# Second layer's modulation vectors by multiply-and-add on VectorE and a matmul against ones

## The chip, the cores and the metric

The kernel runs on one core of one Trainium2 chip. The metric is the device time of one execution in microseconds (us), given as the median of several runs. The engines have short names in the profile: PE is TensorE's matmul, PEld its weight load, DVE VectorE, ACT ScalarE, POOL GpSimd, SP the engine whose queue issues most of the loads.

## The reference

The program is two trunk layers over 512 latent tokens and 256 context tokens, width 1024, all in fp32. Each layer first turns two condition vectors (one for the latent stream, one for the context stream) into six modulation vectors of 1024 numbers per stream:

```python
def modulation(cvec, w_mod, b_mod):
    m = (jax.nn.silu(cvec) @ w_mod + b_mod)[..., None, :]
    return jnp.split(m, 6, axis=-1)

sh1, sc1, ga1, sh2, sc2, ga2 = modulation(c, w_mod, b_mod)
sh1c, sc1c, ga1c, sh2c, sc2c, ga2c = modulation(c_ctx[None], w_mod, b_mod)
u = (rmsnorm(x, g_mix) * (1 + sc1) + sh1) @ w_in
uc = (rmsnorm(cx, g_mix) * (1 + sc1c) + sh1c) @ w_in
...
x = x + ga1 * mix
x = x + ga2 * squared_relu_mlp(rmsnorm(x, g_mlp) * (1 + sc2) + sh2, w_up, w_down)
if update_ctx:      # all layers but the last
    ...             # the same two lines for cx, with ga1c, sc2c, sh2c, ga2c
return x, cx
```

So the modulation is a vector of 1024 numbers times a matrix of 1024 x 6144, for each of two streams, 25 MB of weights a layer. In the second layer the context needs its first shift and scale alone (sh1c, sc1c), because its tokens are not updated there.

## The kernel before

The two layers run one after the other: norm and input projection, three mixing groups, output projection, then the MLP (hidden width 4096, in eight blocks of 512). Every projection on TensorE takes three fp32r matmuls per tile (high by high, high by low, low by high), so each weight tile is loaded raw by SP, rounded to its high part on ACT (line 144), and its low part is the difference on DVE (line 68, called from 145). The raw tiles have three buffers, the high parts five (tag "hi"), the low parts five (tag "lo").

The second layer's modulation is computed during the first layer's MLP. A generator, `mod_all` (361), makes three rounds of 2048 columns: round 0 gives the first shift and scale, round 1 ga1 and the second shift, round 2 the second scale and ga2. `modulation_round` (166) has eight steps in each round, one per tile of 128 rows of w_mod (k). A step loads two tiles of 128 x 1024 (512 KB each) into a "hi" and a "lo" buffer and issues four fp32 matmuls of 512 columns, one for each 32 columns of the array: stationary is a 128 x 32 tile in which columns 0 and 1 hold the two activated condition vectors (`sstat`), moving is the weight tile. The four sums lie on four groups of 32 partitions of one PSUM tile, `pm`. After the eighth step the bias is added (181), four PE transposes (184) make it feature-major, and from round 1 on the gates are written to DRAM (191).

In each of the eight MLP blocks (1152) four up-projections of 128 hidden features are made, and after each of them the generator is advanced by one step (1179). Then comes the down-projection of the block before (1181): per token tile two groups of twelve matmuls, whose result is multiplied by the gate on DVE (1130) and added to the stream on POOL (1131). There are 32 advances; the generator yields 24 times. After the loop it is run out (1183), the next layer's first weights are loaded (1185), and the last down-projection runs with the next layer's norms between its tiles (1193).

The program is written in one order, and a planner (switched on at line 1269) places the instructions on the engines' queues by that order and by its own simulated timeline; on the chip every queue runs in the order so fixed. A buffer's next load waits until its last readers are done.

Of the kernel before, what the change touches and what calls it, by code (L numbers as in the profile page):

```python
# [10 lines left out]
F32 = mybir.dt.float32  # L11
# [3 lines left out]
ALU = mybir.AluOpType  # L15
# [18 lines left out]
def hybrid_kernel(ctx, tc, x, c, cx, c_ctx, w_mod, b_mod, g_mix, w_in, w_pool, s_pool, w_gate, b_gate,  # L34
# [36 lines left out]

# [1 line left out]
    crow = slot("crow", w=128)[0:32]  # L73
# [3 lines left out]
    ident = const.tile([128, 128], F32, name="ident")  # L77
    make_identity(nc, ident)
    mhalf = const.tile([128, 1], F32, name="mhalf")
    V.memset(mhalf, -0.5)  # L80
# [28 lines left out]

    # parameter vectors, feature-major: 23 rows per layer  # L110
    NV = 23
# [15 lines left out]

# [1 line left out]
    def wload(*srcs, sl=False):  # L129
        """columns of all srcs [128, a, *] side by side, as (hi, lo)"""  # L130
        shp = [128, srcs[0].shape[1], sum(s_.shape[2] for s_ in srcs)]
        n = shp[1] * shp[2]
        raw = wp.tile([128, n], F32, tag="raw", name=nm("raw"), bufs=3)
        rv = raw.rearrange("p (a b) -> p a b", b=shp[2])
        o = 0
        for s_ in srcs:
            nc.sync.dma_start(rv[:, :, o:o + s_.shape[2]], s_)
            o += s_.shape[2]
        if sl:
            hi, lo = slot("whi", F32R, w=n), slot("wlo", F32R, w=n)  # L140
        else:
            hi = wp.tile([128, n], F32R, tag="hi", name=nm("whi"))
            lo = wp.tile([128, n], F32R, tag="lo", name=nm("wlo"))
        A.activation(hi, raw, AF.Copy)  # L144
        sub_lo(lo, raw, hi)
        return hi.rearrange("p (a b) -> p a b", b=shp[2]), lo.rearrange("p (a b) -> p a b", b=shp[2])

    def wcols(w, c0, n, ksplit, *more, sl=False):
        """columns c0:c0+n (and of more ranges) of w [1024, *] as KT-tiles; returns f(k) -> (hi, lo) [128, n]"""
        parts = []  # L150
        step = KT // ksplit
        for s in range(ksplit):
            parts.append(wload(*(w[s * step * 128:(s + 1) * step * 128, a:a + m].rearrange("(k p) n -> p k n", p=128)
                                 for a, m in ((c0, n),) + more), sl=sl))
        return lambda k: (parts[k // step][0][:, k % step], parts[k // step][1][:, k % step])

    def wrows(w, r0):
        """128 rows from r0 of w [*, 1024]"""
        hi, lo = wload(w[r0:r0 + 128, :].rearrange("p (a n) -> p a n", a=1))
        return hi[:, 0], lo[:, 0]  # L160

# [1 line left out]
    gaD = dp.tile([2, 2, 2, D], F32, name="gaD")  # L163
    xD = dp.tile([NL, D], F32, name="xD")

    def modulation_round(l, r, modT):
        pm = psC("pm")
        for k in range(KT):
            yield
            for h in range(2):  # L170
# [3 lines left out]
                for j in (2 * h, 2 * h + 1):  # L174
                    T.matmul(pm[32 * j:32 * j + 32, :], sstat[:, k, :], raw[:, (j % 2) * 512:(j % 2) * 512 + 512],  # L175
                             start=(k == 0), stop=(k == KT - 1), skip_group_check=True)
        brow = lay.tile([128, 512], F32, tag="brow", name=nm("brow"))
        for j in range(4):
# [7 lines left out]
        if r >= 1:  # L186
            which = r - 1
            for s in range(2):
                for jj in range(2):
                    row = 32 * (jj + (2 if r == 2 else 0)) + s  # L190
                    nc.scalar.dma_start(gaD[l, which, s:s + 1, jj * 512:(jj + 1) * 512], brow[row:row + 1, :])

    def mod_vec(modT, idx, s):
        """feature-major [128, 8] of modulation vector idx (0..5) for stream s"""
        r, j0 = idx // 2, (idx % 2) * 2
        return modT[:, r, j0:j0 + 2, :, s]
# [5 lines left out]

# [1 line left out]
    def rstd_of(ss, n, tag, post=None):  # L204
        w = ss.shape[1]
        r = mp.tile([128, w], F32, tag=tag, name=nm(tag))
        if w == 1:
            G.tensor_scalar(r, ss, 1.0 / n, EPS, ALU.mult, ALU.add)
            G.tensor_tensor(r, r, mhalf, ALU.pow)
            return r  # L210
        # first guess by exp and log, then a Newton step for 1/sqrt
        u = mp.tile([128, w], F32, tag=tag + "u", name=nm(tag))
# [16 lines left out]
    def norm_pair(p2, X, hT, sc, sh, psf):  # L229
        """token tiles 2*p2 and 2*p2+1 normalised, modulated, transposed into hT hi/lo"""  # L230
        pair = (2 * p2, 2 * p2 + 1)
# [32 lines left out]
    def fm_matmul(ps, wk, hT, nk, lat, ctxs, k0=0, k1=None):  # L264
        """feature-major: weights stationary, tokens moving into ps (latent 0:512, context 512:768)"""
        for k in range(k0, k1 or nk):
# [9 lines left out]
    def fm_pair(ps, wk, hT, nk, p2):  # L276
        """fm_matmul for the two token tiles 2*p2 and 2*p2+1"""
        cs = slice(p2 * 256, p2 * 256 + 256)
# [4 lines left out]
    def tm_matmul(ps, t, wk, hT, nk, c0=0, n=None, k0=0, k1=None):  # L283
        """token-major: tokens of tile t stationary, weights moving"""
        for k in range(k0, k1 or nk):
# [6 lines left out]

# [1 line left out]
    def layer_tables(l, ta):  # L294
        """tables of the mixing half"""
        L = {}
# [50 lines left out]
    def merge(main, other, ratio):  # L347
        """emit main, with `ratio` steps of other after each of its steps; returns what is left of other"""
        acc = 0.0
        for _ in main:  # L350
            acc += ratio
            while acc >= 1.0:
                acc -= 1.0
                next(other, None)
# [6 lines left out]
    def mod_all(l, M):  # L361
        yield from modulation_round(l, 0, M[0])
        fin_scale(l, M, 0)
        yield from mod_rest(l, M)

    X = None
    MODS = [None, None]
    for l in range(2):
# [9 lines left out]
        if l == 0:  # L378
# [16 lines left out]

            # shift and scale of the first norm, features h*256 .. h*256+256; even and odd k apart
            pms = {}
# [122 lines left out]

# [1 line left out]
        mods = mod_rest(0, MODS[0]) if both else iter(())  # L522
# [11 lines left out]

        # gla q, k feature-major, per pair of heads; token-major values and low-rank decay features
        gq, gk = [None, None], [None, None]
# [31 lines left out]
        if l == 0:  # L568
            qk_proj(1, 0)
            qk_proj(1, 1)  # L570
        # decay features r^T
        rT = gp.tile([32, NT], F32, tag="gt", name=nm("rT"), bufs=7)
# [14 lines left out]
        def gate_proj(pr):  # L587
            """silu(gate) * g_gla, feature-major"""
            wk = wcols(W, C_GG + pr * 128, 128, 1)
# [13 lines left out]
        def gla_thread():  # L603
# [32 lines left out]
            def states(pr):  # L636
                """states before each chunk: order ctx 4,5 then latent 0..3 (forward), reversed (backward)"""
                k_ = gk[pr]
# [36 lines left out]
            def levels(pr):  # L675
                """intra-chunk scores A^T[j, i], level by level; from block size 16 on only the diagonal 32-blocks,
                kept side by side"""
                q_, k_ = gq[pr], gk[pr]
# [61 lines left out]
            def outputs(pr):  # L740
# [3 lines left out]
                for d in range(2):  # L744
# [3 lines left out]
                    qe.append(t_)  # L748
                # o^T: the two heads on 64 partitions each
                ps = psA("o")  # L750
# [44 lines left out]

        # attention projections, token-major: Uq[cb][g] q of 4 heads for tiles 3g..3g+2, UK normalised keys,
        # Uv[g] values as (vh, vl) per kv head
        Uq = [[None, None], [None, None]]
# [11 lines left out]
        def rope_mult(v, tab, tmp, nt, nh):  # L810
            """rotate v [128, nt, nh, 64] with tables [C*g, S*swap(g)]"""
            for half in range(2):
# [8 lines left out]
        def head_norm(v, sq, nh, post=None):  # L821
            """v [128, nh, 64] times rsqrt(mean square)"""
            A.activation(sq, v, AF.Square)
# [64 lines left out]

# [1 line left out]
        mixT = [None] * KT  # L890
# [36 lines left out]

        # keys: [kh; kh] and [kl; kl] per kv head
        kst = []
# [12 lines left out]

        # a unit is two query tiles of a pair of heads (of one kv head)
        nunits = 0
# [5 lines left out]
        def softmax_part(n, hp, q0, P):  # L950
            """P gets the unnormalised probabilities by head and tile, and the reciprocal sums"""
            kh, kl = kst[hp // 2]
# [31 lines left out]
        def value_part(n, hp, q0, P):  # L984
# [4 lines left out]
            for ki, kt in enumerate(kts):  # L989
# [13 lines left out]
                yield  # L1003
            # times the reciprocal sums, one per query, on the 64 partitions of each head
            rb_ = psB("rb")
# [55 lines left out]
        at_, att_ = a_thread(), att_thread()  # L1061
        # the order of the steps: gated linear attention, other projections, modulation, softmax attention
        ths = {"g": gla_thread(), "a": at_, "m": mods, "t": att_}
# [11 lines left out]

# [1 line left out]
        xstack = ExitStack()  # L1077
# [40 lines left out]

# [1 line left out]
        ga = [load_ga(l, 1, s) for s in range(2 if both else 1)]  # L1120
# [73 lines left out]
        else:  # L1194
            # final norm, tile by tile
            gf = bp.tile([128, D], F32, tag="ga", name="gf", bufs=2)
# [76 lines left out]
```

## Time and profile before

| what | value |
|---|---|
| timed runs | 1719.51, 1723.79, 1723.97 us; median 1723.79 |
| span of the profiled execution | 1719.9 us, from first to last instruction |
| PE busy | 1639.1 us, 95% |
| DVE, ACT, POOL busy | 866.9, 656.9, 480.3 us |
| mean granted PE clock | 0.980 |

The page gives no time of the profiled execution beside its span; the span lies inside the range of the timed runs, 3.9 us under their median. Times in the trace are counted from the span's start. A row of the chain of waits has start, length and what ran; a row of the timeline has start, length, engine, line, operation, tiles and shape, a count, and in brackets the idle time before it with what ended it; a row of the stretches has for each engine the busy time and the number of instructions, then the granted PE clock, the DMA share and GB/s.

### The profile page before, as it was taken

Reading aid. Unit: us, or ns where it says so; the run is one execution under the profiler, and the core shown is the slowest. Engines: PE = TensorE matmul, PEld = TensorE weight load, DVE = VectorE, ACT = ScalarE, POOL = GpSimd, SP = SyncE. Lnnn points to the kernel's source line nnn. Section 1 sums busy time; section 2 is a strip of 40 time slices with the busy share of each in tenths; the row PEclk is TensorE's granted clock in tenths of the full one; section 3 lists DMA queues with packets and bytes.
Section 4 is the critical chain, followed back from the end, with each engine's and each line's share of the span. In section 5 each row is a group of like instructions: output and inputs, shape, how many; then the busy total and the mean of one; then the engine's idle time right before and its main releaser. Section 6 shows DMA issues by size and latency. Waiting matters only on the chain.

```text
span 1719.9 us, 28685 instructions
## 1 busy us (share of the span) xinstructions
PE 1639.1 (95%) x12059; PEld 1337.3 (78%) x12059; DVE 866.9 (50%) x1209; ACT 656.9 (38%) x1136; POOL 480.3 (28%) x514
## 2 busy tenths in 40 slices
PE   7999797999999999999999999898899999999997
PEld 4988655669987887877888888696568888888885
DVE  4447758643543334333353454767764555445554
ACT  5445356662432113122131134646663432222222
POOL 1104535202301220312313263244312212222225
PEclk9999899999999999999999999898999999999999
DMA  9422340203343415334131222200014233333331
GB/s 309 131 85 75 136 161 3 100 27 122 111 138 96 153 50 184 120 94 147 50 122 56 68 89 75 72 2 2 2 74 130 79 99 98 99 98 98 98 98 49
DMA packets 140256, 163.38 MB, mean 95 GB/s; under 512 B 9412, under 2 KB 116304, under 8 KB 140128
## 3 DMA queue, kind: packets, MB, share of 16 engines
q1 hardware_dynamic: 133312, 147.10, 26.9%
q10 hardware_dynamic: 6816, 14.46, 2.3%
q8 instruction: 94, 1.54, 0.4%
q14 instruction: 34, 0.28, 0.0%
HBM read 157.31 MB, written 4.23 MB: 94 GB/s over the span
## 4 chain that ended last, share of the span: by engine, by line
PE 85%; DVE 5%; POOL 3%; DMA 2%; ACT 2%; issue 2%; SPq 0%; ACTq 0%; POOLq 0%; DVEq 0%
PE dn L291 25%; PE up L272 19%; PE op L291 7%; PE tm L291 6%; PE up L274 5%; PE fm L272 4%; PE av L1001 3%; PE pT L992 2%; PE pm L175 2%; PE up L281 2%; PE fm L274 2%; DMA rawm<-in_w_mod_dram 1%; PE sc L974 1%; PE att L722 1%; PE sc L975 1%
## 5 line engine op out<-in xcount | busy, mean ns | idle before, releaser
L144 ACT ACTIVATE whi<-raw 128x1024 fp32r<-128x1024 f32 (+2 forms) x182 | 184.8, 1031 | 582.2 <-PE dn L291 310.3
L1131 POOL TENSOR_TENSOR X<-X,rtmp 128x512 f32<-128x512 f32 x158 | 218.0, 1384 | 660.9 <-DVE rtmp L1130 660.6
L68 DVE TENSOR_TENSOR wlo<-raw,whi 128x1024 fp32r<-128x1024 f32 (+2 forms) x182 | 225.5, 1247 | 279.0 <-ACT whi L144 273.7
L291 PE MATMUL dn<-whi,ah 128*128 128x512 f32 x640 | 249.8, 390 | 0.4 <-DVE rtmp L1130 0.4
L291 PE MATMUL dn<-whi,al 128*128 128x512 f32 x640 | 249.1, 389 | 0.0
L291 PE MATMUL dn<-wlo,ah 128*128 128x512 f32 x640 | 246.8, 389 | 0.0
L1130 DVE TENSOR_TENSOR rtmp<-dn,ga 128x512 f32<-128x512 f32 x160 | 109.2, 689 | 231.4 <-PE dn L291 229.8
L272 PE MATMUL up<-h2h,whi 128*128 128x512 f32 x464 | 183.8, 396 | 0.7 <-ACT relu L1173 0.7
L272 PE MATMUL up<-h2l,whi 128*128 128x512 f32 x464 | 182.5, 393 | 0.0
L272 PE MATMUL up<-h2h,wlo 128*128 128x512 f32 x464 | 182.5, 393 | 0.0
L291 PEld LDWEIGHTS dn<-whi,ah 128*128 128x128 f32 x640 | 120.1, 188 | 29.8 <-ACT whi L144 4.2
L291 PEld LDWEIGHTS dn<-wlo,ah 128*128 128x128 f32 x640 | 120.1, 188 | 25.0
L291 PEld LDWEIGHTS dn<-whi,al 128*128 128x128 f32 x640 | 120.1, 188 | 24.5
L272 PEld LDWEIGHTS up<-h2h,whi 128*128 128x128 f32 x464 | 87.1, 188 | 31.4 <-ACT relu L1173 7.6
L272 PEld LDWEIGHTS up<-h2l,whi 128*128 128x128 f32 x464 | 87.1, 188 | 21.1 <-issue 1.7
L291 PE MATMUL tm<-whi,hTh 128*128 128x256 f32 (+1 forms) x352 | 102.6, 292 | 0.0
L272 PEld LDWEIGHTS up<-h2h,wlo 128*128 128x128 f32 x464 | 87.1, 188 | 19.6
L291 PE MATMUL tm<-whi,hTl 128*128 128x256 f32 (+1 forms) x352 | 101.3, 288 | 0.0
L291 PE MATMUL tm<-wlo,hTh 128*128 128x256 f32 (+1 forms) x352 | 100.5, 287 | 0.0
L291 PE MATMUL op<-whi,mixh 128*128 128x256 f32 x320 | 91.2, 285 | 0.9 <-ACT whi L144 0.9
L291 PE MATMUL op<-wlo,mixh 128*128 128x256 f32 x320 | 90.2, 284 | 0.3 <-DVE wlo L68 0.3
L291 PE MATMUL op<-whi,mixl 128*128 128x256 f32 x320 | 90.5, 283 | 0.0
(287 smaller groups left out, 3318.7 us busy)
## 6 DMA issues: line engine op xcount, KB each, us to landing
rawm<-in_w_mod_dram SPq DMA_DIRECT2D x80, 512.0 KB
raw<-in_w_up_dram SPq DMA_DIRECT2D x64, 512.0 KB
raw<-in_w_down_dram SPq DMA_DIRECT2D x64, 512.0 KB
raw<-in_w_in_dram SPq DMA_DIRECT2D x26, 512.0 KB
rawm<-in_w_mod_dram SPq DMA_DIRECT2D x32, 256.0 KB
raw<-in_w_out_dram SPq DMA_DIRECT2D x16, 512.0 KB
raw<-in_w_in_dram SPq DMA_DIRECT2D x12, 256.0 KB
ga<-gaD ACTq DMA_DIRECT2D x6, 512.0 KB
```

The source lines that it names most:

```text
L68: V.tensor_tensor(lo, full, hi.bitcast(F32), ALU.subtract)
L144: A.activation(hi, raw, AF.Copy)
L175: T.matmul(pm[32 * j:32 * j + 32, :], sstat[:, k, :], raw[:, (j % 2) * 512:(j % 2) * 512 + 512], start=(k == 0), stop=(k == KT - 1), skip_ ...
L272: T.matmul(ps[:, 0:NL], a, b[:, 0:NL], start=st, stop=sp_)
L274: T.matmul(ps[:, NL:NT], a, b[:, NL:NT], start=st, stop=sp_)
L281: T.matmul(ps[:, cs], a, b[:, cs], start=(k == 0 and i == 0), stop=(k == nk - 1 and i == 2))
L291: T.matmul(ps, a[:, sl], bb, start=(k == 0 and i == 0), stop=(k == nk - 1 and i == 2))
L722: T.matmul(ps[g * bw:(g + 1) * bw, o0:o0 + bw], xk[rows, j0:j0 + bw], xq[rows, i0:i0 + bw], start=True, stop=True)
L992: T.transpose(pt_[:, i * 128:(i + 1) * 128], p_[:, ki * 128:(ki + 1) * 128], ident)
L1001: T.matmul(av_[64 * hh:64 * hh + 64, 0:256], vst, pe[:, hh * 256:hh * 256 + 256], start=(ki == 0), stop=(ki == len(kts) - 1))
L1130: V.tensor_tensor(tmp, ps, ga[0 if t < 4 else 1][:, sl], ALU.mult)
L1131: (V if b == NB - 1 and not both and t == 3 else G).tensor_tensor(X[t][:, sl], X[t][:, sl], tmp, ALU.add)
```

## The change

For the second layer, `mod_all` calls a new generator, `modulation_sums`. It goes through one half (1024 columns) of a round at a time. For each of the eight tiles of rows it loads one tile of w_mod and, for each stream, multiplies it by the condition vector (one number per partition) and adds it to an accumulator of 128 x 1024: the first tile on ACT, as a scaled copy, the other seven on DVE, in one instruction each. After the eighth tile a matmul sums the accumulator over its partitions: stationary is a 128 x 32 tile that has ones in the stream's column and zeros elsewhere (`osel`), and two column groups take 512 columns each. Round 0 has both streams and yields at every tile; rounds 1 and 2 have the latent stream alone and yield at every second tile. That is 16 + 8 + 8 = 32 yields. Bias, transposes and gates are as before, moved into `mod_end`. The accumulators lie in two buffers that the norms use too (tag "xn"). The first layer's modulation is as it was. Comments are emptied.

```diff
+    osel = const.tile([128, 2, 32], F32, name="osel")
+    V.memset(osel, 0.0)
+    for s in range(2):
+        V.memset(osel[:, s, s:s + 1], 1.0)
...
+        mod_end(l, r, modT, pm)
+
+    def mod_end(l, r, modT, pm):
         brow = lay.tile([128, 512], F32, tag="brow", name=nm("brow"))
...
+    def modulation_sums(l, r, modT, streams):
+        pm = None
+        for h in range(2):
+            acc = [bp.tile([128, 1024], F32, tag="xn", name=nm("macc"), bufs=2) for _ in range(streams)]
+            c0 = r * 2048 + h * 1024
+            for k in range(KT):
+                if k % 2 == 0 or streams == 2:
+                    yield
+                raw = wp.tile([128, 1024], F32, tag="lo" if k % 2 else "hi", name=nm("rawm"))
+                nc.sync.dma_start(raw, w_mod[l, k * 128:(k + 1) * 128, c0:c0 + 1024])
+                for s in range(streams):
+                    c_ = sstat[:, k, s:s + 1]
+                    if k == 0:
+                        A.activation(acc[s], raw, AF.Copy, scale=c_)
+                    else:
+                        V.scalar_tensor_tensor(acc[s], raw, c_, acc[s], ALU.mult, ALU.add)
+            if pm is None:
+                pm = psC("pm")
+            for s in range(streams):
+                for j in (2 * h, 2 * h + 1):
+                    T.matmul(pm[32 * j:32 * j + 32, :], osel[:, s], acc[s][:, (j % 2) * 512:(j % 2) * 512 + 512],
+                             start=(s == 0), stop=(s == streams - 1), skip_group_check=True)
+        mod_end(l, r, modT, pm)
...
     def mod_all(l, M):
-        yield from modulation_round(l, 0, M[0])
+        yield from modulation_sums(l, 0, M[0], 2)
         fin_scale(l, M, 0)
-        yield from mod_rest(l, M)
+        yield from modulation_sums(l, 1, M[0], 1)
+        yield from modulation_sums(l, 2, M[0], 1)
+        fin_scale(l, M, 1)
```

## The prediction

> **What bounds the kernel now.** I read the page first: its shares, its slices of PE, its chain of waits.
>
> ```profile
> span 1719.9 us, 28685 instructions
> PE 1639.1 (95%) x12059; PEld 1337.3 (78%) x12059; DVE 866.9 (50%) x1209; ACT 656.9 (38%) x1136; POOL 480.3 (28%) x514
> PE   7999797999999999999999999898899999999997
> ...
> PE 85%; DVE 5%; POOL 3%; DMA 2%; ACT 2%; issue 2%; SPq 0%; ACTq 0%; POOLq 0%; DVEq 0%
> ```
>
> The kernel is bound by PE nearly everywhere. The change lies in the first layer's MLP, so I took stretches of it next: an MLP block with modulation steps and one without (columns: PE, PEld, DVE, ACT, POOL busy and counts, clock, DMA share, GB/s).
>
> ```profile
> 754.00:825.00 71.00, 71.00 (x372) 56.91 (x368) 24.78 (x28) 14.25 (x17) 16.30 (x12) 1.00 0.36 119
> ...
> 893.00:960.00 67.00, 67.00 (x341) 56.81 (x340) 26.38 (x28) 14.44 (x16) 16.38 (x12) 1.00 0.17 51
> ```
>
> PE is busy in every one of the 71.00 and 67.00 us, at clock 1.00, while DVE, ACT and POOL have more than half of each block free. A microsecond that PE doesn't work there is a microsecond of the kernel, as long as no wait takes its place. What a modulation step costs is read from the starts of the down-projections in the chain:
>
> ```profile
> 754.76 8.38 PE dn L291 x36
> ...
> 825.96 8.38 PE dn L291 x36
> ...
> 893.90 32.68 PE dn L291 x144
> ...
> 960.50 53.05 PE dn L291 x234
> ```
>
> From 754.76 to 825.96 is 71.20 us, a block with four steps; from 893.90 to 960.50 is 66.60, a block with none. The difference of 4.60 is 1.15 a step. The chain around one step agrees:
>
> ```profile
> 581.58 0.24 PE up L272
> 581.94 0.99 PE pm L175 x8
> 582.94 0.43 PE up L272
> ```
>
> The step itself takes 0.99, and the first matmul behind it 0.43 where its like takes 0.24.
>
> **The change part by part.** *Removed:* 24 steps by 1.15 = 27.6 us of PE.
>
> *Added on PE:* the ones-matmuls have the removed ones' shape. In these timeline rows a whole step (eight records, two per matmul, four column groups) takes 1.06 and half a step (four records, two groups) 1.05, so groups run side by side and a pair alone costs what four did:
>
> ```profile
> 134.57 1.06 PE L175 MATMUL pm<-rawm,sstat 128*32 128x512 f32 x8
> 136.12 1.05 PE L175 MATMUL pm<-rawm,sstat 128*32 128x512 f32 x4 [0.49 <-DMA rawm<-in_w_mod_dram]
> ```
>
> Rounds 1 and 2 have four such pairs, 4 x 1.15 = 4.6. Round 0 has two halves of two streams, and the second stream goes through the same column groups, so it comes behind the first: 1.15 + 0.99 = 2.14 each, 4.3 together. Sum 8.9; bounds 4 x 1.05 + 2 x (1.05 + 0.99) = 8.3 and 8 x 1.15 = 9.2. The transposes and the bias at the three rounds' ends stay. PE's balance is -27.6 + 8.9 = **-18.7 us**.
>
> *Added on DVE and ACT:* 7 x 2 halves x (2 + 1 + 1) = 56 multiply-and-adds of 128 x 1024 on DVE, and 8 scaled copies on ACT. The nearest rows:
>
> ```profile
> L68 DVE TENSOR_TENSOR wlo<-raw,whi 128x1024 fp32r<-128x1024 f32 x170 | 213.9, 1266 | 273.5 <-ACT whi L144 268.5 <-PE pm L175 2.3 <-ACT pe L996 1.9
> L144 ACT ACTIVATE whi<-raw 128x1024 fp32r<-128x1024 f32 x170 | 177.3, 1057 | 572.4 <-PE dn L291 310.3 <-PE up L274 69.7 <-PE op L291 42.9
> L622 DVE SCALAR_TENSOR_TENSOR e<-z 128x768 f32<-128x768 f32 x8 | 7.6, 954 | 2.1 <-ACT z L621 2.1
> ```
>
> ```profile
> L1212 DVE SCALAR_TENSOR_TENSOR y<-X,rstd,gf x4: 751/1574/1770, 1704.2 to 1715.2; 128x512 f32<-128x512 f32 x4
> ```
>
> The same operation takes 0.954 on 768 columns, so 1.27 on 1024; the difference of two tiles of the very size takes 1.266. I take 1.27: 71 us, 8.9 a block, which brings DVE from 24.8 to 33.7 of some 68. The upper bound is the last row's median of 1.574 on 512 columns (behind POOL's work at the end), 3.15 on 1024: 176 us, 22 a block, 47 of 68. Even that fits; the cover is DVE's 46 idle us a block, and without it the 71 us would stand against the 18.7. ACT's eight copies cost 8 x 1.06 = 8.5 over all blocks, beside 14 of 71 busy. I put both at 0 on the path, with a loss only through order (rivals).
>
> A timeline pair shows POOL and DVE in each other's way: the gated sum takes 1.29 alone, and 2.20 where it falls on a low-part subtraction.
>
> ```profile
> 573.75 1.29 POOL L1131 TENSOR_TENSOR X<-X,rtmp 128x512 f32<-128x512 f32 x1 [1.43 <-DVE rtmp L1130]
> 577.09 2.20 POOL L1131 TENSOR_TENSOR X<-X,rtmp 128x512 f32<-128x512 f32 x1 [2.05 <-DVE rtmp L1130]
> ```
>
> [...]
>
> *Moved:* the 48 loads of 512 KB stay 48, but go by halves and reach into the seventh and eighth block. Their queue waits for buffers:
>
> ```profile
> SPq L173 <- PE dn L291: 153.1, 17, 29.5
> ...
> SPq L173 <- PE pm L175: 29.1, 11, 8.5
> ```
>
> ```profile
> 858.70 0.81 SPq L173 DMA_DIRECT2D rawm<-in_w_mod_dram  x2
> ...
> 937.13 29.85 SPq L137 DMA_DIRECT2D raw<-in_w_in_dram  x4
> ```
>
> The tile is now given back by DVE instead of by PE's place in line; the wait on the step's matmuls (29.1) goes, the one on the down-projections (153.1) stays, since they hold four of five "hi" buffers. The last loads now stand ahead of the next layer's first weights in SP's queue, which are issued from 937.13, while PE is in down-projections until 960.50 + 53.05 = 1013.6; those 76 us cover a load or two of 3.63 us (a row of the second rival). The round ends with four bias loads and four small stores on ACT's queue and the bias sum on DVE; these move later by one to two blocks, still ahead of their readers in the second layer. I take 0.
>
> *The new constant:* three memsets on DVE at the start, beside these rows.
>
> ```profile
> 0.97 0.27 DVE L98 MEMSET sstat<- 128x256 f32 x1
> ...
> 3.56 0.19 DVE L102 COPY cvec<-pcv 128x32 f32<-128x32 f32 x1 [1.86 <-PE pcv L100]
> ```
>
> They cost at most 3 x 0.27 and lie before DVE's idle 1.86 us; 0, or 0.8 without that cover.
>
> **Sum.** 1719.9 - 18.7 = 1701.2 us of span. The median of the timed runs is 3.9 above that span, so I forecast **1705 us**. Its own range is 1702 to 1710: the matmul bounds of -0.6 and +0.3, up to 3 for waits at the six groups of ones-matmuls, which now hang on DVE, and some 2 of scatter between the runs (1719.5 to 1724.0).
>
> **The rivals.** *The removed step was a cover.* At a block's turn to its down-projection the fourth down weight is made just in time:
>
> ```profile
> 539.35 1.06 ACT L144 ACTIVATE whi<-raw 128x1024 fp32r<-128x1024 f32 x1 [5.61 <-PE up L274]
> ```
>
> ```profile
> 540.44 1.23 DVE L68 TENSOR_TENSOR wlo<-raw,whi 128x1024 fp32r<-128x1024 f32 x1 [5.57 <-ACT whi L144]
> ...
> 556.66 0.69 DVE L1130 TENSOR_TENSOR rtmp<-dn,ga 128x512 f32<-128x512 f32 x1 [2.03 <-PE dn L291]
> ...
> 582.82 0.96 DVE L1175 TENSOR_TENSOR relu<-relu 128x768 f32<-128x768 f32 x1 [4.68 <-ACT relu L1173]
> ```
>
> ```profile
> 540.54 0.50 PE L291 MATMUL dn<-whi,ah 128*128 128x512 f32 x1
> ...
> 543.16 0.39 PE L291 MATMUL dn<-wlo,ah 128*128 128x512 f32 x1
> ```
>
> Its buffer comes free with the last up-projection; copy and difference end at 541.67, and PE reads it at 543.16 at the latest, 1.5 later. Without the step's 1.0 in between the margin is 0.5; with one multiply-and-add of 1.27 ahead of the difference it is -0.8, two make it -2.0. Paid in all eight blocks at -0.8 to -1.5 that is 6 to 12 us given back: 1711 to 1717, say 1713. Against it: in the block without steps (893 to 960) the same turn has no gap, and PE has up-projections of the next block to slip in.
>
> *DVE's queue is held by loads (slower).* The multiply-and-add waits for its tile at the head of DVE's queue, and behind it stand the next low parts, the squared ReLU and the gate products that empty PSUM. A load that nobody fetched ahead takes this long in the chain:
>
> ```profile
> 132.45 3.63 DMA rawm<-in_w_mod_dram
> ```
>
> There are 32 steps, so it decides from 18.7 / 32 = 0.58 us of PE idle per step on. If a step holds DVE for 3.63 and the 2.03 us that DVE idles between two gate products (row 556.66) don't cover all of it, 1.0 to 1.6 reach PE: 32 to 51 us, 13 to 32 slower, 1737 to 1756, say 1740. For it: the chip runs the planner's order, fixed on simulated landing times. Against it: PE, which stands at the head of such loads now, idles 0.9 us in all for them (the next row), and DVE has 4.68 us free where a block's up-projections begin (row 582.82).
>
> ```profile
> L175 PE MATMUL pm<-rawm,sstat 128*32 128x512 f32 x320 | 46.6, 614 | 0.9 <-DMA rawm<-in_w_mod_dram 0.9
> ```
>
> [...]
>
> *Nothing is gained:* PE's freed time turns into waits of 0.4 to 0.75 us at each of 32 steps, 13 to 24 us, by either way; then 1718.6 to 1729, say 1722. For it speaks only that a PE-bound plan with new dependences is re-planned as a whole, the second layer included.
>
> **How the numbers follow.** About 0.3%, 5.2 us, is what a measurement of this kernel can tell from no change. I give the forecast 0.66, the lost cover 0.16, nothing gained 0.08, the held queue 0.10. Faster by over 0.3% (under 1718.6) is the first two, 0.82; within it 0.08; slower 0.10. The range of 1701 to 1717 holds the forecast and nearly all of the lost cover.
>
> **What would show it.** After: no matmul with `sstat` past the first layer's mixing half; ones-matmuls of 8.1 to 9.2 us in six groups; blocks of 66.6 us, plus 1.15 to 2.3 where a group falls; DVE at 32 to 36 us a block; multiply-and-adds of 1.2 to 1.35 each. The lost cover would show as PE idle on the low part at each start of a down-projection; the held queue as DVE idle on modulation loads, with PE waiting for DVE behind them. I am wrong if blocks stay above 69 us or the passage into the second layer grows by more than 3 us.

## The result, and the profile after

The changed kernel takes **1703.76 us** in the median of four runs (1700.82 to 1706.90). The kernel before, with one more run beside it on the same chip, has 1723.88 (1719.51 to 1725.69). The ratio of the runs is 0.9892, with a 95% interval of 0.9874 to 0.9910: about 1.1% faster, or 15.5 to 21.7 us of 1723.88.

The profiled execution after is the slowest of its four (1706.9). Its span is 1704.9, 2.0 us less than its time. First the page after, the lines that answer to those of before.

```profile
span 1704.9 us, 28454 instructions
...
PE 1620.6 (95%) x11899; PEld 1337.4 (78%) x11899; DVE 947.5 (56%) x1268; ACT 666.0 (39%) x1144; POOL 477.7 (28%) x514
...
PE 84%; DVE 5%; POOL 3%; ACT 3%; issue 2%; DMA 2%; SPq 0%; ACTq 0%; POOLq 0%; DVEq 0%
```

PE's busy time fell from 1639.1 to 1620.6, by 18.5 us; DVE's rose from 866.9 to 947.5, by 80.6. The chain is still PE's by 84%. The kernel is bound as before, with less to do on PE and more on DVE.

Next the MLP blocks in the view of stretches, from one start of a down-projection to the next (columns as in the prediction: PE, PEld, DVE, ACT, POOL busy and counts, granted clock, DMA share, GB/s).

```profile
536.90:605.50 68.60, 68.60 (x346) 56.81 (x345) 34.61 (x34) 16.64 (x19) 16.37 (x12) 1.00 0.29 92
605.50:672.10 66.60, 66.60 (x338) 56.46 (x337) 36.78 (x36) 14.43 (x17) 16.37 (x12) 1.00 0.31 95
672.10:740.70 68.60, 68.60 (x349) 57.18 (x349) 35.75 (x41) 15.66 (x18) 16.37 (x12) 1.00 0.37 119
740.70:808.40 67.70, 67.70 (x341) 56.50 (x340) 35.64 (x35) 15.73 (x18) 15.46 (x12) 1.00 0.37 125
```

PE is busy in every microsecond of each block, at clock 1.00. A block without ones-matmuls takes 66.60, the same as the block without steps before. Blocks that had 71 now have 66.6 to 68.6. DVE went from 24.8 us a block to between 34.6 and 36.8, and PE lost nothing by it here. What the groups of ones-matmuls cost stands in the chain of waits (start, length, what ran):

```profile
578.03 1.84 PE pm L223 x8
605.51 32.66 PE dn L325 x144
672.09 32.65 PE dn L325 x144
...
740.67 32.68 PE dn L325 x144
782.17 0.98 PE pm L223 x4
808.44 32.65 PE dn L325 x144
```

A half of round 0 with both streams takes 1.84, and its block is 2.0 longer than 66.6; a pair of one stream takes 0.98, and the block from 740.67 to 808.44 is 1.2 longer. The groups of instructions show what each new operation takes (count, busy time, mean ns of one, idle time before it and what ended it):

```profile
L218 DVE SCALAR_TENSOR_TENSOR macc<-rawm,sstat,macc 128x1024 f32<-128x1024 f32 x56 | 75.7, 1371 | 8.6 <-DMA rawm<-in_w_mod_dram 7.7 <-ACT macc L216 0.7
L216 ACT ACTIVATE macc<-rawm,sstat 128x1024 f32<-128x1024 f32 x8 | 9.1, 1148 | 13.3 <-DMA rawm<-in_w_mod_dram 12.6 <-PE ptr L277 0.5 <-PE pm L223 0.2
L223 PE MATMUL pm<-macc,osel 128*32 128x512 f32 x32 | 8.0, 601 | 0.0
```

The multiply-and-adds did wait for loads, 7.7 us in all, but nothing on PE stood behind that.

**Where the time came from.** I measure the MLP from the first layer's first up-projection on PE to the pair of gate products on DVE at the passage into the second layer. Before, from a timeline row and a row of the chain:

```profile
459.06 0.28 PE L281 MATMUL up<-h2h,whi 128*128 128x256 f32 x1
...
1029.92 1.27 DVE rtmp L1130 x2
```

After:

```profile
461.00 0.28 PE L315 MATMUL up<-h2h,whi 128*128 128x256 f32 x1
...
1015.48 1.27 DVE rtmp L1166 x2
```

The stage went from 570.86 to 554.48: **16.4 us** were gained there. From the second row to the span's end it is 690.0 before and 689.4 after, so the second layer takes as long as it did. The early part is 1.9 longer in the profiled run after (461.00 against 459.06); over the profiled executions of the table below, the last one aside, its end scatters from 459.1 to 462.4, though the program up to there differs by three memsets at most. So spans fell by 15.0 between the two profiled executions, and medians by 20.1. The stage is the measure for all that follows: it is free of the early part's scatter, and e8_first_layer, which leaves it alone, repeats it to 0.02 (554.50). That the medians fell by 3.7 more than the stage lies within the interval of the ratio (15.5 to 21.7); no trace shows where it comes from.

The balance of the prediction was 18.7. The stage gives 16.4, so **2.3 us are missing**, and nearly all of them lie at one place. The first block's up-projections begin while the MLP norm of the context tiles is still running. The stretch from the first up-projection to the first one of 512 columns had three steps, 3 x 1.15 = 3.45. Before, the row of the stretch, and PE's waits in it (us in total, times, the longest):

```profile
459.06:485.06 26.00, 25.03 (x195) 20.65 (x193) 16.11 (x29) 13.67 (x26) 8.86 (x11) 1.00 0.53 163
```

```profile
PE up L272 <- ACT relu L1173: 0.7, 1, 0.7
PE up L281 <- POOL h2l L256: 0.3, 1, 0.3
```

After:

```profile
461.00:485.75 24.75, 20.79 (x170) 19.97 (x169) 19.66 (x31) 15.47 (x28) 8.99 (x11) 1.00 0.38 112
```

```profile
PE up L306 <- ACT relu L1209: 1.5, 1, 1.5
PE up L315 <- DVE h2l L290: 1.4, 1, 1.4
PE up L315 <- POOL h2l L290: 0.6, 1, 0.6
PE up L315 <- ACT h2h L285: 0.5, 1, 0.5
```

PE's work fell by 4.24 us (25.03 to 20.79), but its idle time rose from 0.97 to 3.96. Of the 3.45 expected, 1.25 arrived; 2.2 of the missing 2.3 are here. Behind the stretch, from 485.75 to 1003, PE is busy without a gap. The stretch had more to give than 3.45, because one of its three steps ran in two halves, and in the chain of before each half takes as long as a whole step:

```profile
476.20 0.98 PE pm L175 x4
...
479.19 1.01 PE pm L175 x4
```

So 4.24 us of work went and 3.0 us of idle time came. What PE waits for is the norm's high and low parts (`h2h`, `h2l`) and the squared ReLU. The chain of waits after, in that stretch, says what these had been waiting for:

```profile
476.99 1.16 ACT macc L216
...
478.18 0.46 DVE macc L218
...
479.45 0.53 DVE full L289
479.99 1.19 DVE macc L218
481.18 0.87 DVE h2l L290
...
482.09 1.82 PE up L315 x13
...
483.94 0.14 ACT whi L149
...
484.90 0.80 ACT relu L1209
```

Scaled copies of the first modulation tile stand ahead of the norm on ACT (476.99, and one more at 478.50), and the first two multiply-and-adds on DVE, between its own instructions. But not every wait is of this kind. By PE's timeline the wait of 0.57 for POOL ends at 475.64, before the first of the new instructions starts. The waits of 0.45 and 1.45 that end at 480.14 and 482.09 come behind them. The last, 1.49 where it was 0.67 before, comes behind the rounding of a weight tile (L149, 483.94, 1.06 long), which the plan now has ahead of the squared ReLU and had behind it before. So 1.9 of the 3.96 us of idle time stand directly behind the new work; of the rest 0.67 was there before, and 1.4 comes with another order of the old work.

### The profile page after: what moved, and what is told of

The parts are those of the page before. It is cut to its first block, busy times and chain, and to the rows that moved or that the text cites. A ratio compares the mean times of both kernels' runs of the same rounds, so it can differ in the third digit from the quotient of the medians.

```text
span 1704.9 us, 28454 instructions
## 1 busy us (share of the span) xinstructions
PE 1620.6 (95%) x11899; PEld 1337.4 (78%) x11899; DVE 947.5 (56%) x1268; ACT 666.0 (39%) x1144; POOL 477.7 (28%) x514
## 3 DMA queue, kind: packets, MB, share of 16 engines
HBM read 157.31 MB, written 4.23 MB: 95 GB/s over the span
## 4 chain that ended last, share of the span: by engine, by line
PE 84%; DVE 5%; POOL 3%; ACT 3%; issue 2%; DMA 2%; SPq 0%; ACTq 0%; POOLq 0%; DVEq 0%
PE dn L325 24%; PE up L306 19%; PE op L325 7%; PE tm L325 6%; PE up L308 5%; PE fm L306 4%; PE av L1037 3%; PE pT L1028 3%; PE up L315 2%; PE fm L308 2%; PE sc L1010 1%; PE att L758 1%; PE pm L180 1%; PE sc L1011 1%; DMA rawm<-in_w_mod_dram 1%
## 5 line engine op out<-in xcount | busy, mean ns | idle before, releaser
L149 ACT ACTIVATE whi<-raw 128x1024 fp32r<-128x1024 f32 (+2 forms) x182 | 185.1, 1032 | 573.4 <-PE dn L325 291.9
```

## The experiments

The first theory (Q) is that the new work stands in the queues of ACT and DVE ahead of the norm, and PE waits for the norm. Its rival (F) is that the removed matmuls were filler: PE would have waited for the norm anyway, and the steps only filled the wait. Both could explain the stretch above; they differ in whether the wait goes when the new work is moved away. A third, that the planner with other work to place has put the old work in a worse order, is not told apart from Q by moving the work, since the plan is then made anew too. In all runs the first stretch and the stage are counted between the same rows as above, and the ratio is to runs of the kernel before on the same chip.

| run | first stretch, us | stage, us | timed median, us (range) | ratio (95%) |
|---|---|---|---|---|
| before | 26.00 | 570.86 | 1723.88 (1719.51 to 1725.69) | |
| the change | 24.75 | 554.48 | 1703.76 (1700.82 to 1706.90) | 0.9892 (0.9874 to 0.9910) |
| e5_late_start | 21.77 | 551.50 | 1701.80 (1699.85 to 1702.98) | 0.9886 (0.9860 to 0.9911) |
| e3_no_sums | 25.28 | 552.31 | 1707.18 (1700.54 to 1708.36) | 0.9890 (0.9845 to 0.9935) |
| e2_round0_old | 26.00 | 556.56 | 1708.30 (1705.71 to 1710.91) | 0.9927 (0.9902 to 0.9952) |
| e1_both_streams | 24.76 | 559.66 | 1711.38 (1710.15 to 1715.50) | 0.9949 (0.9932 to 0.9966) |
| e6_late_no_sums | 21.76 | 550.24 | 1700.09 (1696.69 to 1704.72) | 0.9862 (0.9838 to 0.9887) |
| e4_together | 25.55 | 554.16 | 1705.75 (1705.14 to 1708.48) | 0.9915 (0.9893 to 0.9938) |
| e7_late_together | 22.02 | 550.19 | 1703.19 (1700.82 to 1704.31) | 0.9885 (0.9865 to 0.9905) |
| e8_first_layer | | 554.50 | 1751.99 (1751.60 to 1753.05) | 1.0171 (1.0152 to 1.0190) |

### e5_late_start: the same work, begun after the norm

The first block advances the generator once instead of four times; the next three blocks make up for it.

```diff
                 act.append((ah, al))
-                next(mods, None)
+                for _ in range(0 if b == 0 and i < 3 else 2 if b in (1, 2, 3) and i == 3 else 1):
+                    next(mods, None)
```

> The change with its first step put off: no advance of the modulation after the first three up-projections of the first MLP block, and one more advance in each of the second to fourth block. The stretch from the first up-projection of the first MLP block to the first of the next 128x512 up-projections (the norm of the context tiles falls into it) took 24.8 us before with three modulation steps in it, and 23.6 after the change with none, so 2.2 us of the three steps' 3.45 came back as PE idle time. Theory Q (queues): the scaled copies on ACT and the sums on DVE stand ahead of the norm's own instructions there. Then this kernel has the stretch at about 21.4 us and the kernel time falls by about 2 us, to 1701.5. Theory F (filler): the removed steps filled idle time in which PE waits for the norm in any case. Then the stretch stays at 23.6 us and the time at about 1703.8.

The first stretch and PE's waits in it:

```profile
461.10:482.87 21.77, 20.64 (x170) 19.93 (x168) 14.85 (x30) 13.02 (x26) 8.41 (x12) 1.00 0.35 98
```

```profile
PE up L306 <- ACT relu L1209: 0.7, 1, 0.7
PE ptr L277 <- DVE xn L270: 0.4, 1, 0.4
```

PE does the same work as in the change (20.64 us against 20.79), and its idle time falls from 3.96 to 1.13. The stretch is 2.98 shorter, and so is the stage (554.48 to 551.50): nothing was given back elsewhere. The expectation counted the stretch from another row, 1.2 us later; on its count the run has 20.6, where theory Q gave 21.4. F, by which the wait would have stayed, falls. Q's forecast is met and passed by 0.8: the squared ReLU, too, now stands ahead of the rounding again, as before, and its wait is back at 0.7. So the new work's early start costs the 3.0 us, by its place in the queues and by the order that came with it; how much by each, the run does not tell. The stretch is now 4.23 shorter than before, all of the 4.24 of work that went, and the stage 19.4, which is 0.7 beyond the balance of 18.7, since the balance took 3.45 for these three steps. The timed medians differ by less than the runs of either kernel scatter, so by the time alone this version can't be told from the change.

### e3_no_sums: which queue, DVE's or ACT's

This kernel leaves out the 56 multiply-and-adds.

```diff
                         A.activation(acc[s], raw, AF.Copy, scale=c_)
-                    else:
-                        V.scalar_tensor_tensor(acc[s], raw, c_, acc[s], ALU.mult, ALU.add)
```

> The change with VectorE's 56 multiply-and-adds left out, the eight scaled copies on ScalarE left where they are (so the second layer's modulation is not the reference's: only the first tile of each half goes into it). Question: which of the two holds the first MLP block's norm of the context tiles, the sums or the copies. The stretch from the first up-projection to the first of 512 columns takes 26.00 us before, 24.75 in the change and 21.77 with the steps moved out of it. If the sums in VectorE's queue hold it, the stretch falls to 22 to 22.8 and the stage from the first up-projection to the passage into the second layer from 554.5 to 551 to 552. If the copies in ScalarE's queue hold it, the stretch stays at 24 to 24.8 and the stage at 553.5 to 554.5. Each alone: between, 22.8 to 24.

The run gives no clean answer on the split. Without sums the accumulators were ready at once, and the plan moved two groups of ones-matmuls into the stretch, where they fill PE's waits. It also put two roundings of weight tiles ahead of the squared ReLU (timeline rows of PE, ACT and PE; the first group, at 479.96, looks like the one shown):

```profile
481.61 1.05 PE L221 MATMUL pm<-macc,osel 128*32 128x512 f32 x4
...
484.34 2.00 ACT L149 ACTIVATE whi<-raw 128x1024 fp32r<-128x1024 f32 x2 [2.52 <-DMA rawm<-in_w_mod_dram]
...
487.09 0.50 PE L304 MATMUL up<-h2h,whi 128*128 128x512 f32 x1 [2.08 <-ACT relu L1207]
```

The stretch is 25.28, or 23.2 without these two matmul groups, in the middle of what the two answers gave; the stage is 552.31, also between them, with some 0.6 lost behind the stretch (51.62 us to the first down-projection, 50.99 in the change), where the 128x512 up-projections from 488.85 to 490.77 took 0.63 each, against 0.40 before and behind. The stage is 2.2 shorter than the change's; the time (1707.18) does not show it. The trace says a little more of the norm itself. Its last low part ends 21.0 us after the first up-projection here, 22.0 in the change and 18.4 in e5_late_start. So without the sums the norm ends 0.9 of those 3.5 us earlier, and the rest is with the copies on ACT, which stand here as in the change, or with the plan's order. How the 3.0 us of e5_late_start divide stays open.

### e2_round0_old: round 0 back on PE

```diff
     def mod_all(l, M):
-        yield from modulation_sums(l, 0, M[0], 2)
+        yield from modulation_round(l, 0, M[0])
         fin_scale(l, M, 0)
```

> Round 0 undone (eight steps with four fp32 matmuls each, as in the kernel before), rounds 1 and 2 by sums: 8 x 1.15 + 4 x 1.15 = 13.8 us of modulation on PE against 8.9 in the change and 27.6 before. Theory of the balance alone: 4.9 us above the change, 1708.7. With the 2.2 us at the first block's norm (either theory, Q or F, since the steps are back there): 2.7 above, about 1706.5. Rival: the gain is not proportional to the matmuls removed but hangs on taking them all out of the blocks: then most of the gain is lost, 1715 or more.

The first stretch is that of the kernel before again, to the last digit of the view:

```profile
460.06:486.06 26.00, 25.03 (x195) 20.65 (x193) 16.11 (x29) 13.67 (x26) 8.86 (x11) 1.00 0.53 163
```

The stage is 2.1 longer than with the change. By the balance alone round 0's eight steps (9.2) against its ones-matmuls (4.3) would be 4.9; the expectation took off 2.2 for the norm, and 2.7 was left. So of the 4.9 that round 0's move to DVE should have brought, 2.8 did not come: 2.2 in the first stretch, where 1.25 is left of the three steps' 3.45, and 0.6 elsewhere. Rounds 1 and 2 alone earn 14.3 against the kernel before, where their balance gives 13.8, so the gain does go with the matmuls removed.

### e1_both_streams: twice the sums in rounds 1 and 2

The second stream's sums, which the second layer doesn't need, are made as well: 28 more multiply-and-adds, four more scaled copies, four more pairs of ones-matmuls.

```diff
-                if k % 2 == 0 or streams == 2:
+                if k % 2 == 0 or r == 0:
                     yield
...
-        yield from modulation_sums(l, 1, M[0], 1)
-        yield from modulation_sums(l, 2, M[0], 1)
+        yield from modulation_sums(l, 1, M[0], 2)
+        yield from modulation_sums(l, 2, M[0], 2)
```

> The change with both streams in rounds 1 and 2 (yields as in the change): 28 more multiply-and-adds on DVE (28 x 1.28 = 36 us), four more copies on ACT, four more pairs of ones-matmuls on PE. Theory B (PE's balance, DVE hidden): 4 x 0.99 = 4.0 us more, about 1707.8; DVE at some 40 of 69 us in the later blocks, PE busy in all of it. Rival D (DVE's work comes through): up to 36 us more, 1740.

```profile
739.40:808.30 68.90, 68.90 (x345) 56.66 (x344) 42.64 (x42) 16.71 (x19) 17.11 (x12) 1.00 0.40 127
```

With 42.64 of DVE's 68.90 us taken, PE is still busy in all of the block. The stage grew by 5.2, of which four pairs at 0.98 are 3.9; so some 36 us more on DVE (28 x 1.28) cost at most 1.3. Behind the first stretch PE waited for DVE for 0.7 us in all, 0.5 of it for the last sums. The timed median grew by 7.6, more than the stage; the profiled spans differ by 3.5 only (1708.4 and 1704.9), so I take no more from the time than its sign.

### e6_late_no_sums: e5_late_start without the sums

```diff
                         A.activation(acc[s], raw, AF.Copy, scale=c_)
-                    else:
-                        V.scalar_tensor_tensor(acc[s], raw, c_, acc[s], ALU.mult, ALU.add)
...
+                for _ in range(0 if b == 0 and i < 3 else 2 if b in (1, 2, 3) and i == 3 else 1):
+                    next(mods, None)
```

> The late start with the 56 multiply-and-adds on DVE left out: the accumulators hold the scaled copy of the first tile alone, so the second layer's modulation is not the reference's; loads, copies and ones-matmuls stay. It prices DVE's 72 us (56 x 1.28) away from the norm. Theory B (hidden behind PE): the MLP stage, 551.5 us with the late start (461.1 to 1012.6), and the time, 1701.8, stay within 1 us. Rival D: some of the 72 us comes through at the turns from up- to down-projection or at the passage into the second layer, and the stage gets shorter by 2 us or more.

The same 475 us in the view of stretches, first e5_late_start, then this run:

```profile
537.00:1012.00 475.00, 475.00 (x2367) 395.88 (x2367) 255.28 (x274) 112.08 (x132) 133.39 (x106) 1.00 0.34 113
```

```profile
537.00:1012.00 475.00, 475.00 (x2372) 396.52 (x2371) 196.07 (x228) 111.88 (x132) 135.48 (x106) 1.00 0.33 113
```

DVE has 59 us less to do, and PE is busy in every microsecond of both. Leaving out all sums shortens the stage by 1.26 (551.50 to 550.24), between the 1 us of theory B and the 2 of its rival. Outside the norm's stretch the sums are hidden but for that 1.3 us at most.

### e4_together: both halves of a round in one group

In rounds 1 and 2 the ones-matmuls of the first half wait for the second, so that four column groups go side by side.

```diff
+            accs.append(acc)
+            if streams == 1 and h == 0:
+                continue
...
-                for j in (2 * h, 2 * h + 1):
-                    T.matmul(pm[32 * j:32 * j + 32, :], osel[:, s], acc[s][:, (j % 2) * 512:(j % 2) * 512 + 512],
+                for j in ((0, 1, 2, 3) if streams == 1 else (2 * h, 2 * h + 1)):
+                    T.matmul(pm[32 * j:32 * j + 32, :], osel[:, s], accs[j // 2][s][:, (j % 2) * 512:(j % 2) * 512 + 512],
```

> The change with rounds 1 and 2 issuing the two halves' ones-matmuls together, after the second half: four column groups side by side instead of two pairs apart. Theory P (a pair alone costs what four groups cost, about 1.0 us and 0.15 at the switch): two groups less, each of 1.15 us, MLP stage and kernel time 2.3 us lower, four groups of 0.98 become two of about 1.0. Rival: a pair costs half of four (0.5): the groups become two of 2.0 and nothing changes.

From its chain of waits:

```profile
850.42 0.99 PE pm L227 x8
...
951.79 0.98 PE pm L227 x4
952.78 2.95 PE dn L329 x12
955.73 0.98 PE pm L227 x4
```

Round 1's eight records take 0.99, as long as four do: four column groups cost what two cost, as in the prediction's rows 134.57 and 136.12. Its two blocks together are 1.63 shorter than in the change (66.59 + 67.73 against 67.77 + 68.18). In round 2 the plan put a piece of the down-projection between the two pairs, and nothing was gained. The stage fell by 0.32 only, since the first block took 1.2 longer up to its down-projection (77.13 against 75.90): PE's granted clock was 0.50 there from 485 to 490, and 1.00 in the change. The run's stretch from 485 to 490, then the change's:

```profile
485.00:490.00 5.00, 3.79 (x14) 3.11 (x14) 5.00 (x6) 3.91 (x5) 0.00 (x0) 0.50 0.59 187
```

```profile
485.00:490.00 5.00, 4.25 (x24) 3.69 (x25) 5.00 (x5) 3.19 (x4) 0.00 (x0) 1.00 0.83 246
```

### e7_late_together: both edits

The edits of e5_late_start and e4_together in one kernel.

> The late start and the halves together in rounds 1 and 2, in one kernel. In the run with the halves together alone, round 1's two pairs went as one group of 0.99 us and round 2's were placed 4 us apart. Theory P: 1.2 us less than the late start for round 1 and nothing for round 2 if its pairs are apart again: stage 550.3 us, time about 1700.6; 2.3 less if both are joined. That would be the fastest of these kernels, though 1.2 us is less than the scatter of the times.

The stage is 550.19, 1.31 less than e5_late_start's, where 1.2 was expected. Behind the norm's stretch of 22.02 the 128x512 up-projections take 0.40 each (from 484.63 on), not the 0.63 that they took at 488.17 in e4_together. This is the shortest stage of a kernel with the whole computation, 20.7 less than before. Its timed median, 1703.19, can't be told from the change's 1703.76 or from e5_late_start's 1701.80.

### e8_first_layer: the same exchange in the first layer

Rounds 1 and 2 of the first layer's modulation, which run during its norm, projection and mixing, go to DVE in the same way, with both streams and accumulators of 128 x 512.

```diff
     def mod_rest(l, M):
-        yield from modulation_round(l, 1, M[0])
-        yield from modulation_round(l, 2, M[0])
+        yield from modulation_slots(1, M[0])
+        yield from modulation_slots(2, M[0])
```

```diff
+                raw = wp.tile([128, 1024], F32, tag="lo" if k % 2 else "hi", name=nm("rawm"))
+                nc.sync.dma_start(raw, w_mod[0, k * 128:(k + 1) * 128, c0:c0 + 1024])
+                for s in range(2):
+                    c_ = sstat[:, k, s:s + 1]
+                    for q in range(2):
+                        rq_ = raw[:, q * 512:q * 512 + 512]
+                        if k == 0:
+                            A.activation(acc[s][q], rq_, AF.Copy, scale=c_)
+                        else:
+                            V.scalar_tensor_tensor(acc[s][q], rq_, c_, acc[s][q], ALU.mult, ALU.add)
```

> The change, and rounds 1 and 2 of the first layer by the same means, both streams, with accumulators of 512 columns (112 multiply-and-adds of 128x512 on DVE, 16 copies on ACT, 16 ones-matmuls in place of 64 fp32 matmuls). They run in the mixing half, where the kernel before has DVE busy 78 of 100 us between 100 and 200 us, and PE 83 to 94 of 100. Theory N (the swap pays only where PE is full and DVE is not): PE gets 16 x 1.1 - 4 x 2.1 = 9 us less, DVE 112 x 0.75 = 84 us more; the first layer's MLP starts 10 us or more later than in the change (462 us), time 1714 or more. Rival G (every matmul taken away pays): it starts up to 9 us earlier, time about 1695.

The time is 1751.99, 48 us more than the change's. All of it lies ahead of the MLP, which begins at 509.36 instead of 461.00 and takes 554.50 as before. Stretch from 200 to 300, the change, then this run:

```profile
200.00:300.00 100.00, 83.71 (x1616) 55.01 (x1616) 65.47 (x111) 54.38 (x111) 41.17 (x53) 0.90 0.28 97
```

```profile
200.00:300.00 100.00, 54.40 (x686) 37.29 (x684) 96.89 (x141) 37.63 (x63) 42.63 (x29) 0.64 0.31 98
```

The view of waits of this run, from 100 to 420 (what PE waited for: us in total, times, the longest):

```profile
PE pm L224 <- DVE macc L218: 12.8, 5, 5.8
```

DVE had 35 of these 100 us free; now it is busy for 97, and PE stands idle for 46 of 100 with a granted clock of 0.64. The exchange paid in the MLP, where in the blocks shown before the change PE was busy throughout and DVE for 24.8 of 71.00 us, and lost here. It is a dearer exchange, though: two streams make 112 multiply-and-adds of half the size for a forecast 9 us of PE. How the 48 us divide between waits, the buffers that the accumulators take and the lower clock is not told apart by these runs.

## Why the prediction was right, and where it was not

- **What bounds the kernel: right.** PE is busy for all of each block shown, before and after.
- **PE's balance of -18.7: right to within 0.8.** PE's busy time fell by 18.5. The step that ran in two halves cost some 1.9 instead of 1.15, since the three of the first stretch came to 4.24; behind the first stretch the stage is 15.1 shorter, where 21 steps at 1.15 less 8.9 give 15.3. Ones-matmuls took 8.0 us by the group's row, just under the 8.1 to 9.2 of the last part, because the two-stream half takes 1.84 and not 2.14; by the blocks' lengths (2.0 and 1.2 over 66.6) they cost what was reckoned.
- **The sums on DVE: size nearly right.** A multiply-and-add was taken as 1.27; the shortest is 1.27, the mean 1.37. The rows in which they take longer lie beside work of POOL, as the 2.34 at 774.82, the 2.19 at 842.72 and the 2.08 at 911.02 on gated sums of 1.28 to 1.29 that POOL began at 774.80, 842.54 and 910.72. All that stands above 1.27 is some 5 us (75.7 against 56 x 1.27 = 71.1). DVE's 34.6 to 36.8 a block lies at the upper edge of "32 to 36" and over it.
- **"I put both at 0 on the path": this is the step that failed.** It holds in the blocks (e6_late_no_sums: 1.3 us at most for all sums). It does not hold where the first three advances fall on the norm of the context tiles: started there, the work costs 2.2 us against the prediction and 3.0 against the same work placed later (e5_late_start). PE waited 1.9 us directly behind copies on ACT (1.15 each, not 1.06) and sums on DVE; the rest came with the order of the plan, a loss "through order" that the prediction left to its rivals but looked for in other places. The prediction took the cover from a block's mean, 25 of 68 us busy; the first block's stretch had DVE busy for 16.11 of 26.00 with a chain through it that PE was waiting for.
- **"Up to 3 for waits at the six groups": a loss of that size came, at another place.** The groups waited for nothing on the path; the norm did.
- **The lost cover at the down-projections** did not show: 68.60 of 68.60 and 66.60 of 66.60 us of the blocks are PE's. Its price was not worked out evenly either: its own margins were -0.8 and -2.0, the sum took -0.8 to -1.5.
- **Nothing is gained** did not come: PE's new idle time is 3.0 us at one place, not 0.4 to 0.75 at each of 32 steps.
- **The held queue** showed as a mechanism, in small. DVE did idle for loads (7.7 us), with no PE wait behind it in the blocks. PE did wait for DVE behind this work, but once, and for the sums themselves rather than for their loads. Its condition, 0.58 us at every step, was far from met in the MLP. In e8_first_layer, where DVE has little room, PE waited 12.8 us for the sums.
- **Moved loads, late ends of the rounds and the memsets at 0: not contradicted.** The second layer takes 689.4 after its start, against 690.0.
- **From span to time:** the prediction added the 3.9 us by which the median stood above the profiled span. In the four runs after, time is span plus 2.0 to 2.1, so some 1.9 of the 3.9 was the scatter of one execution. That the forecast of 1705 came within 1.3 of 1703.76 is in part luck: the gain in the stage was 2.3 less than forecast, and the medians fell by more than the stage.

## What to carry to other kernels

When PE is bound and another engine is half idle, the exchange can be worth the PE time that it frees, and that can be read off the distance between repeated rows of the chain; here 18.5 us of PE time went for 75.7 us of DVE work. Whether the other engine's work was free here was not a matter of its mean: begun in a stretch in which PE waited for a chain through that engine, the same work cost 3.0 us more than begun after it (24.75 against 21.77). So look for such a stretch, and start the new work after it. In the one case tried where that engine was already busy for two thirds of the time (65.47 of 100 us), the exchange lost 48 us.

## What the runs showed of the hardware

In e4_together PE's granted clock was 0.50 from 485 to 490 us, though no single wait of PE there exceeded 1.46 us. Its timeline rows of PE with a wait between 482 and 489:

```profile
482.91 0.39 PE L319 MATMUL up<-h2l,whi 128*128 128x256 f32 x1 [1.46 <-DVE h2l L294]
487.36 0.79 PE L310 MATMUL up<-h2h,whi 128*128 128x512 f32 x1 [1.21 <-ACT relu L1213]
```

The matmul at 487.36 took 0.79, where its like in the change, at 485.75, took 0.50. The change has nearly the same waits at the same place (1.45 and 1.49) and kept 1.00. The sum of the short waits does not explain the 0.50 alone: from 480 to 490 PE was idle for 3.12 us here and for 3.08 in the change. In e3_no_sums, a little behind a wait of 2.08 that ended at 487.09, 128x512 up-projections took 0.63 from 488.85 to 490.77, as at 488.17 here. What sets it off stays open.
